# Row-wise dot products of two streamed arrays: another split of the last step between VectorE and ScalarE, other transfer sizes at its end, and all sums of six steps on VectorE

## The chip, the cores and the metric

The kernel runs on one core of one Trainium2 chip. The metric is the device time of one execution in microseconds, the median of several runs. The core's engines named here are VectorE (DVE in the profile), ScalarE (ACT) and SyncE (SP, which issues most of the transfers). TensorE (PE) and GpSimd (POOL) do no work of the kernel's own. Sixteen DMA engines move data between HBM and SBUF.

## What is computed

`x` and `y` are float32 of shape (8, 4096, 512). For each batch the reference forms the full product `x @ y^T`, takes its diagonal and a softmax over the 4096 diagonal values:

```
gram = np.matmul(x, y.transpose(0, 2, 1))
diag = np.diagonal(gram, axis1=1, axis2=2)
diag = diag - diag.max(axis=-1, keepdims=True)
exp = np.exp(diag)
return (exp / exp.sum(axis=-1, keepdims=True)).astype(np.float32)
```

Only the diagonal is needed, so the kernel computes 8 x 4096 dot products of 512 elements, row of `x` with the same row of `y`, and then the softmax of each batch. It reads 134 MB and writes 0.13 MB.

## The kernel before

The 128 partitions hold four batches of 32 partitions each; a partition has 128 consecutive rows of its batch. So the eight batches are two sets of four, and a set is 128 rows per partition. The rows are worked on in eight **steps** (0 to 7) of 32 rows per partition, four steps to a set. One step's `x` or `y` is 16384 elements, 64 KB, per partition. The results of a set are the 128 columns of `diag[0]` or `diag[1]`.

**Buffers.** `x` has two buffers, `xs0` and `xs1`, used in turn; `y` has one, `ys`. All input goes through SyncE's queue in the order of the program. An `x` transfer of step t+2 waits until the sums of step t have read their buffer, a `y` transfer of step t+1 until the products of step t have read `ys`.

**Steps 0 to 5** (L133 to L144). ScalarE copies the last K = 6 rows of `y` into `side` (L136). VectorE multiplies rows 0 to 25 of `x` by `ys` in place (`products`, L78), which frees `ys` for the next transfer, then rows 26 to 31 by `side`. VectorE then sums rows 0 to 29 in one reduction (`sums`, L81), and ScalarE the last W = 2 rows, one instruction with an accumulator for each (`sums_act`, L86). After step 3 the first set's maximum and exponentials follow (`exps`), and in step 4 its normalization (`normalize`).

**Step 6** (L146 to L156). The same with other sizes: three products of 8, 9 and 15 rows, the middle one from a copy of `y` in the free end of the other `x` buffer. VectorE sums the last two rows and ScalarE the first 30.

**Step 7** (L159 to L187). Its rows arrive in pieces, `x` and `y` in turn: x 15 rows, y 17, x 8, y 9, x 6, y 3, y 1, in the loop that begins at L164. Behind each piece VectorE takes the rows of which both sides are then asked for, one fused product and sum for each (`dots` and `dot`, L89). After row 16 it takes the maximum over the 48 values that set 1's steps 6 and 7 have so far (`largest`, L106). Then come `x` from row 29 up to all but the last V = 320 elements of row 31 (L179), y row 30, y row 31, and the last V elements of `x` (L185). Row 31 is taken in two parts of 192 and 320 elements. The first part's sum is written into the element of `x`'s buffer behind the row; `ys` has a 1.0 there, so that the second dot product, over 321 elements, adds it.

**The end.** ScalarE copies the finished part of `diag[1]` to `met` (L189), a copy that nothing reads; it stands ahead of the exponential and takes ScalarE's waits for earlier results. SyncE writes the first set's results in six transfers (L192). Each waits until an earlier transfer of the same semaphore has landed; eight semaphores are used in turn, so which one a transfer waits for depends on its place in the order. Then come the maximum over the last values, over the 32 partitions of each batch (L100), exponential and sum (L113), sum over the 32 partitions, reciprocal and scaling (L119, L120), and the output of set 1 from ScalarE's queue (L194).

Of the kernel before, what the change touches and what calls it, by code (L numbers as in the profile page):

```python
# [11 lines left out]
def kernel(  # L12
# [6 lines left out]
    nc = tc.nc  # L19
    ctx.enter_context(tc.manual_schedule())  # L20
    f32 = mybir.dt.float32
    Alu = mybir.AluOpType
    Act = mybir.ActivationFunctionType
    X = mybir.AxisListType.X
    B, N, D = x.shape
    P = nc.NUM_PARTITIONS
    G = 32
    Q = P // G
    C = N // G
    R = 32  # L30
    H = R // 2
    K = 6
    W = 2
    F = H + 1
    L = 9
    E = 64
    V = 5 * D // 8
    U = D - V
    S = B // Q * (C // R)

# [6 lines left out]
    small = ctx.enter_context(tc.tile_pool(name="small", bufs=1))  # L47
# [6 lines left out]
    ys = yflat[:, : R * D].rearrange("p (r d) -> p r d", d=D)  # L54
    side = big.tile([P, K, D], f32, name="side")

    diag = [small.tile([P, C + 2 * i], f32, name=f"diag{i}") for i in range(B // Q)]
# [6 lines left out]
    def rows(t, r0, n):  # L64
        return xs[t % 2][:, r0 : r0 + n, :]

    def dots_of(t, r0, n):
        return diag[t * R // C][:, columns(t, r0, n)]

    def load_x(t, r0, n):  # L70
        nc.sync.dma_start(out=rows(t, r0, n), in_=xv[t * R // C, :, columns(t, r0, n), :])  # L71

    def load_y(t, r0, n):
        nc.sync.dma_start(out=ys[:, r0 : r0 + n, :], in_=yv[t * R // C, :, columns(t, r0, n), :])  # L74

    def products(t, r0, n, yt):
        xt = rows(t, r0, n)
        nc.vector.tensor_tensor(out=xt, in0=xt, in1=yt, op=Alu.mult)  # L78

    def sums(t, r0, n):  # L80
        nc.vector.tensor_reduce(out=dots_of(t, r0, n), in_=rows(t, r0, n), axis=X, op=Alu.add)  # L81

    def sums_act(t, r0, n):
        for r in range(r0, r0 + n):
            row = xs[t % 2][:, r, :]
            nc.scalar.activation(out=row, in_=row, func=Act.Copy, accum_out=dots_of(t, r, 1))  # L86

    def dot(xt, yt, out):
        nc.vector.scalar_tensor_tensor(  # L89
            out=xt, in0=xt, scalar=1.0, in1=yt, op0=Alu.mult, op1=Alu.mult, accum_out=out  # L90
        )

    def dots(t, r0, n):
        for r in range(r0, r0 + n):
            dot(xs[t % 2][:, r, :], ys[:, r, :], dots_of(t, r, 1))

    def over_quadrant(name, column, op, negate=False):

        got = small.tile([P, 1], f32, name=name)
        nc.vector.tensor_reduce(  # L100
            out=got, in_=column.to_broadcast([P, G]), axis=X, op=op, negate=negate, apply_transpose=True
        )
        return got

    def largest(out, d):
        nc.vector.tensor_reduce(out=out, in_=d, axis=X, op=Alu.max)  # L106

    def exps(i, d):
        mxp = small.tile([P, 1], f32, name=f"mxp{i}")
        largest(mxp, d)  # L110
        nmx = over_quadrant(f"nmx{i}", mxp, Alu.max, negate=True)
        sump = small.tile([P, 1], f32, name=f"sump{i}")
        nc.scalar.activation(out=res[i], in_=diag[i][:, :C], func=Act.Exp, bias=nmx, scale=1.0, accum_out=sump)  # L113
        return sump

    def normalize(i, sump):
        total = over_quadrant(f"sum{i}", sump, Alu.add)
        rc = small.tile([P, 1], f32, name=f"rc{i}")
        nc.vector.reciprocal(out=rc, in_=total)  # L119
        nc.vector.tensor_single_scalar(out=res[i], in_=res[i], scalar=rc, op=Alu.mult)  # L120
# [12 lines left out]
    for t in range(S - 2):  # L133
        load_x(t, 0, R)
        load_y(t, 0, R)
        nc.scalar.activation(out=side, in_=ys[:, R - K :, :], func=Act.Copy)  # L136
        if t == C // R:
            normalize(0, sump)
        products(t, 0, R - K, ys[:, : R - K, :])
        products(t, R - K, K, side)  # L140
        sums(t, 0, R - W)
        sums_act(t, R - W, W)
        if t == C // R - 1:
            sump = exps(0, diag[0])  # L144

    t = S - 2  # L146
# [13 lines left out]
    chained = xflat[t % 2][:, R * D : R * D + 1]  # L160
    late = R * D - V
    upto = {load_x: 0, load_y: 0}
    done = 0
    for load, n in (  # L164
        (load_x, H - 1), (load_y, F), (load_x, 8), (load_y, 9), (load_x, 6), (load_y, 3), (load_y, 1)
    ):
        load(t, upto[load], n)
        upto[load] += n
        both = min(upto.values())
        dots(t, done, both - done)  # L170
        done = both
        if done == F:
            largest(diag[1][:, C : C + 1], diag[1][:, C - 2 * R : C - R + H])

    first = (R - 3) * D
    xt = xflat[t % 2]
    xrow = xv[t * R // C].rearrange("p c d -> p (c d)")
    end = ((t % (C // R)) + 1) * R * D
    nc.sync.dma_start(out=xt[:, first : late], in_=xrow[:, end - R * D + first : end - V])  # L179
    dots(t, done, 1)  # L180
    load_y(t, R - 2, 1)
    dots(t, R - 2, 1)
    load_y(t, R - 1, 1)
    dot(xt[:, late - U : late], yflat[:, late - U : late], chained)
    nc.sync.dma_start(out=xt[:, late : R * D], in_=xrow[:, end - V : end])  # L185
    dot(xt[:, late : R * D + 1], yflat[:, late : R * D + 1], dots_of(t, R - 1, 1))

    met = small.tile([P, C - R], f32, name="met")
    nc.scalar.activation(out=met, in_=diag[1][:, : C - R], func=Act.Copy)  # L189

    for p, n in ((0, H), (H, H), (2 * H, H), (3 * H, H), (4 * H, 2 * H), (6 * H, 2 * H)):
        nc.sync.dma_start(out=ov[0, p : p + n, :], in_=res[0][p : p + n, :])  # L192
    normalize(1, exps(1, diag[1][:, C - R + H :]))
    nc.scalar.dma_start(out=ov[1], in_=res[1])  # L194


# [28 lines left out]
```

## Time and profile before

| | |
|---|---|
| median of 3 runs | 319.96 us (319.86 to 320.12) |
| span of the profiled execution | 318.4 us |
| VectorE busy | 241.7 us, 76% of the span |
| ScalarE busy | 49.8 us, 16% |
| HBM read, written | 134.22 MB, 0.13 MB; 422 GB/s over the span |

The profiled execution is one run more, and its span is from the first to the last instruction; a time of its own beside the span isn't given, so the median stands for it: 1.56 us lie around the span. In the rows of the profile, L78 is line 78 of the kernel before. A row of the order of time has the start in us, the duration in us, the engine (SPq is SyncE's queue), the line, the operation and "out<-in". In brackets stands how long the engine was idle before it and what ended that. A row of a group has the operation, its shapes, how often it ran, then busy us and mean ns of one, then the idle time before.

### The profile page before, as it was taken

The page shows a single profiled execution, that of the slowest core. Times are in us where ns is not written, and L with a number is a line of the kernel's source. Part 1 is how long each engine was busy: PE and PEld are TensorE (multiplying, and loading weights), DVE is VectorE, ACT ScalarE, POOL GpSimd, SP SyncE. Part 2 cuts the span into 40 slices and gives each one's busy share as a digit, 9 for nine tenths or more (in the row PEclk, how much of TensorE's full clock was granted, in tenths as well). Part 3 has the DMA queues.
Part 4 walks back from the last instruction along what each step waited for, and adds up shares of the span by engine and source line. Part 5 has one row for each costly group of instructions (what it writes and reads, how often), then busy time and mean ns, then how long its engine had stood idle before and what let it go on. Part 6 is the DMA issues. An engine that isn't in the chain of part 4 may idle for free.

```text
span 318.4 us, 320 instructions
## 1 busy us (share of the span) xinstructions
DVE 241.7 (76%) x101; ACT 49.8 (16%) x97; POOL 0.2 (0%) x4
## 2 busy tenths in 40 slices
DVE  0000079994899939999399994999939998499995
ACT  1000030100301003010020102101030100496700
POOL 0000000000000000000000000000000000000000
DMA  9999999999999999999999999999999999999993
GB/s 397 395 395 510 412 395 453 469 395 395 486 436 395 453 469 395 395 486 436 395 395 519 403 395 461 461 395 395 527 395 395 486 436 395 425 415 432 434 410 140
DMA packets 3970, 134.37 MB, mean 422 GB/s; under 512 B 512, under 2 KB 896, under 8 KB 1536
## 3 DMA queue, kind: packets, MB, share of 16 engines
q1 hardware_dynamic: 3824, 134.29, 97.9%
q10 hardware_dynamic: 144, 0.07, 0.1%
q14 instruction: 2, 0.02, 0.0%
HBM read 134.22 MB, written 0.13 MB: 422 GB/s over the span
## 4 chain that ended last, share of the span: by engine, by line
DMA 70%; DVE 28%; issue 0%; SPq 0%; ACT 0%; DVEq 0%
DMA ys<-in_y_dram 59%; DVE xs L78 28%; DMA xs<-in_x_dram 11%; DVE xs L89 0%; SPq L74 0%; SPq L71 0%; DVE res L120 0%; DVE nmx L100 0%; DVE sum L100 0%; ACT res L113 0%; DVE mxp L106 0%; DVE rc L119 0%; DVEq L78 0%; DVEq L89 0%; SPq L131 0%
## 5 line engine op out<-in xcount | busy, mean ns | idle before, releaser
L78 DVE TENSOR_TENSOR xs<-xs,ys 128x13312 f32<-128x13312 f32 (+2 forms) x8 | 96.7, 12091 | 70.3 <-DMA ys<-in_y_dram 70.3
L81 DVE TENSOR_REDUCE diag<-xs 128x30 f32<-128x15360 f32 (+1 forms) x7 | 98.1, 14020 | 0.2
L86 ACT ACTIVATE xs<-xs 128x512 f32<-128x512 f32 x42 | 25.9, 617 | 90.4 <-DVE xs L78 90.4
L136 ACT ACTIVATE side<-ys 128x3072 f32<-128x3072 f32 x6 | 16.6, 2763 | 124.5 <-DMA ys<-in_y_dram 124.5
L89 DVE SCALAR_TENSOR_TENSOR xs<-xs,ys 128x512 f32<-128x512 f32 (+2 forms) x33 | 20.0, 669 | 0.8 <-DMA ys<-in_y_dram 0.7
L78 DVE TENSOR_TENSOR xs<-xs,side 128x3072 f32<-128x3072 f32 x6 | 20.1, 3350 | 0.0
L86 ACT ACTIVATION_READ_ACCUMULATOR xs<-xs 128x1 f32 x42 | 7.8, 187 | 0.0
L150 ACT ACTIVATE xs<-ys 128x4608 f32<-128x4608 f32 x1 | 4.0, 4043 | 19.9 <-DMA ys<-in_y_dram 19.9
L113 ACT ACTIVATE res<-diag,nmx 128x128 f32<-128x128 f32 x2 | 0.8, 401 | 29.8 <-DVE nmx L100 29.8
L78 DVE TENSOR_TENSOR xs<-xs,xs 128x4608 f32<-128x4608 f32 x1 | 5.0, 4951 | 0.0
L89 DVE DVE_READ_ACCUMULATOR xs<-xs,ys 128x1 f32 x33 | 2.7, 81 | 0.0
L124 ACT ACT_TABLE_LOAD x1 | 1.3, 1283 | 0.7 <-PEq L209 0.7
L100 DVE TRANSPOSE_TENSOR_REDUCE sum<-sump 128x1 f32<-128x32 f32 x2 | 0.4, 212 | 1.2 <-ACT res L113 1.2
L128 DVE MEMSET ys<- 128x1 f32 x1 | 0.1, 59 | 1.4 <-PEq L209 1.4
L120 DVE TENSOR_SCALAR res<-res,rc 128x128 f32<-128x128 f32 x2 | 0.6, 286 | 0.1
L106 DVE TENSOR_REDUCE mxp<-diag 128x1 f32<-128x128 f32 (+1 forms) x2 | 0.5, 228 | 0.1
L100 DVE TRANSPOSE_TENSOR_REDUCE nmx<-mxp 128x1 f32<-128x32 f32 x2 | 0.4, 212 | 0.1
L106 DVE TENSOR_REDUCE diag<-diag 128x1 f32<-128x64 f32 (+1 forms) x2 | 0.4, 202 | 0.0
L119 DVE RECIPROCAL rc<-sum 128x1 f32<-128x1 f32 x2 | 0.3, 164 | 0.1
L113 ACT ACTIVATION_READ_ACCUMULATOR res<-diag,nmx 128x1 f32 x2 | 0.4, 186 | 0.0
L189 ACT ACTIVATE met<-diag 128x96 f32<-128x96 f32 x1 | 0.3, 282 | 0.0
L209 POOL MEMSET const-bfloat16-1.0<- 128x1 bf16 x1 | 0.1, 101 | 0.0
(3 smaller groups left out, 0.3 us busy)
## 6 DMA issues: line engine op xcount, KB each, us to landing
ys<-in_y_dram SPq DMA_DIRECT2D x1, 4352.0 KB, 14.8
xs<-in_x_dram SPq DMA_DIRECT2D x1, 3840.0 KB, 14.1
ys<-in_y_dram SPq DMA_DIRECT2D x1, 2304.0 KB, 12.2
xs<-in_x_dram SPq DMA_DIRECT2D x1, 2048.0 KB, 19.3
xs<-in_x_dram SPq DMA_DIRECT2D x1, 1536.0 KB, 15.5
ys<-in_y_dram SPq DMA_DIRECT2D x1, 768.0 KB, 16.9
ys<-in_y_dram SPq DMA_DIRECT2D x3, 256.0 KB, 18.2
xs<-in_x_dram SPq DMA_DIRECT2D x1, 608.0 KB, 18.0
```

Source lines behind the costliest of these rows:

```text
L78: nc.vector.tensor_tensor(out=xt, in0=xt, in1=yt, op=Alu.mult)
L81: nc.vector.tensor_reduce(out=dots_of(t, r0, n), in_=rows(t, r0, n), axis=X, op=Alu.add)
L86: nc.scalar.activation(out=row, in_=row, func=Act.Copy, accum_out=dots_of(t, r, 1))
L89: nc.vector.scalar_tensor_tensor(out=xt, in0=xt, scalar=1.0, in1=yt, op0=Alu.mult, op1=Alu.mult, accum_out=out)
L100: nc.vector.tensor_reduce(out=got, in_=column.to_broadcast([P, G]), axis=X, op=op, negate=negate, apply_transpose=True)
L106: nc.vector.tensor_reduce(out=out, in_=d, axis=X, op=Alu.max)
L113: nc.scalar.activation(out=res[i], in_=diag[i][:, :C], func=Act.Exp, bias=nmx, scale=1.0, accum_out=sump)
L119: nc.vector.reciprocal(out=rc, in_=total)
L120: nc.vector.tensor_single_scalar(out=res[i], in_=res[i], scalar=rc, op=Alu.mult)
L124: nc.scalar.preload_act_table(Act.Exp)
L136: nc.scalar.activation(out=side, in_=ys[:, R - K :, :], func=Act.Copy)
L150: nc.scalar.activation(out=spare, in_=ys[:, F - L : F, :], func=Act.Copy)
```

## The change

- In steps 0 to 5 VectorE sums all 32 rows; ScalarE's two row sums go.
- In step 7 rows 0 to 9 are no longer dot products: VectorE makes two products of five rows each (2560 elements), and ScalarE sums the ten rows.
- The y of rows 26 to 29 comes in one transfer of four rows instead of three and one.
- V, the part of row 31 that arrives last, is 256 elements instead of 320 (the first part 256 instead of 192).
- The maximum so far is taken after row 25 instead of row 16, so that the last one runs over 6 + 2 values instead of 16 + 2.
- `met` copies the ten columns of ScalarE's sums too.
- The first set's results go out in seven transfers instead of six.

```
-    V = 5 * D // 8
+    V = D // 2
+    A = 10
...
-        sums(t, 0, R - W)
-        sums_act(t, R - W, W)
+        sums(t, 0, R)
...
-    for load, n in (
-        (load_x, H - 1), (load_y, F), (load_x, 8), (load_y, 9), (load_x, 6), (load_y, 3), (load_y, 1)
-    ):
+    for load, n in ((load_x, H - 1), (load_y, F), (load_x, 8), (load_y, 9), (load_x, 6), (load_y, 4)):
         load(t, upto[load], n)
         upto[load] += n
         both = min(upto.values())
+        if done < A <= both:
+            for r in range(0, A, A // 2):
+                products(t, r, A // 2, ys[:, r : r + A // 2, :])
+            sums_act(t, 0, A)
+            done = A
         dots(t, done, both - done)
         done = both
-        if done == F:
-            largest(diag[1][:, C : C + 1], diag[1][:, C - 2 * R : C - R + H])
+        if load is load_x and done > F:
+            seen = done
+            largest(diag[1][:, C : C + 1], diag[1][:, C - 2 * R : C - R + seen])
...
-    dots(t, done, 1)
+    dots(t, R - 3, 1)
...
-    met = small.tile([P, C - R], f32, name="met")
-    nc.scalar.activation(out=met, in_=diag[1][:, : C - R], func=Act.Copy)
-
-    for p, n in ((0, H), (H, H), (2 * H, H), (3 * H, H), (4 * H, 2 * H), (6 * H, 2 * H)):
+    met = small.tile([P, C - R + A], f32, name="met")
+    nc.scalar.activation(out=met, in_=diag[1][:, : C - R + A], func=Act.Copy)
+
+    for p, n in ((0, H), (H, H), (2 * H, H), (3 * H, H), (4 * H, H), (5 * H, H), (6 * H, 2 * H)):
...
-    normalize(1, exps(1, diag[1][:, C - R + H :]))
+    normalize(1, exps(1, diag[1][:, C - R + seen :]))
```

## The prediction, made before the result was known

> **What bounds the kernel now.** I read the page's totals first, then the chain of waits, then the order of time in one step and at the end, then the landings of the last step's transfers.
>
> ```profile
> span 318.4 us, 320 instructions
> DVE 241.7 (76%) x101; ACT 49.8 (16%) x97; POOL 0.2 (0%) x4
> DMA  9999999999999999999999999999999999999993
> ```
>
> VectorE (DVE) is busy 76% of the span and ScalarE (ACT) 16%, but the 16 DMA engines stand at nine tenths or more in every slice but the last. The kernel is a stream of transfers with a short tail, so two questions decide: does the change open a gap in the stream, and what does it do to the tail?
>
> The profiled execution spans 318.4 us; the median of the runs is 319.96 us, 1.56 us more, which lies around the span. I leave that part as it is and add my sum to both.
>
> One step, in order of time (step 0's work, with the issues for steps 1 and 2):
>
> ```profile
> 56.17 0.33 SPq L74 DMA_DIRECT2D ys<-in_y_dram  x1
> 59.39 16.15 DVE L81 TENSOR_REDUCE diag<-xs 128x30 f32<-128x15360 f32 x1
> 75.61 0.33 SPq L71 DMA_DIRECT2D xs<-in_x_dram  x1
> 80.89 14.03 DVE L78 TENSOR_TENSOR xs<-xs,ys 128x13312 f32<-128x13312 f32 x1 [5.35 <-DMA ys<-in_y_dram]
> 269.53 0.33 SPq L71 DMA_DIRECT2D xs<-in_x_dram  x1
> ```
>
> SyncE issues the x of step 2 when the sums of step 0 are done, at 75.61. At that time the y of step 1 is still on its way: VectorE starts on it at 80.89, after 5.35 us of idling. So the queue has about 5 us of work when the next x is put behind it. The tightest place is the x for step 7, issued at 269.53, with the y of step 6 landing at 250.11 + 24.41 = 274.52 (next fence): a lead of 5.0 us.
>
> The end, from the chain of waits:
>
> ```profile
> 250.11 24.41 DMA ys<-in_y_dram
> ...
> 298.80 14.80 DMA xs<-in_x_dram
> ...
> 313.70 0.51 DVE xs L89 x2
> 314.23 0.18 DVE mxp L106
> ```
>
> The last transfer, x's last 320 elements, lands at 298.80 + 14.80 = 313.60; the last dot product starts at 313.70, and maximum, exponential, sum, scaling and the output follow it. All of that tail stays as it is in the change but for two sizes.
>
> Now the last step's transfers: SyncE's issues, then kilobytes and the time from issue to landing.
>
> ```profile
> 292.00 0.33 SPq L74 DMA_DIRECT2D ys<-in_y_dram  x1
> 292.38 0.43 SPq L71 DMA_DIRECT2D xs<-in_x_dram  x1
> 292.85 0.43 SPq L74 DMA_DIRECT2D ys<-in_y_dram  x1
> 293.33 0.43 SPq L74 DMA_DIRECT2D ys<-in_y_dram  x1
> 293.80 0.43 SPq L179 DMA_DIRECT2D xs<-in_x_dram  x1
> 294.75 0.43 SPq L74 DMA_DIRECT2D ys<-in_y_dram  x1
> ```
>
> ```profile
> ys<-in_y_dram SPq DMA_DIRECT2D x1, 2304.0 KB, 12.2
> xs<-in_x_dram SPq DMA_DIRECT2D x1, 1536.0 KB, 15.5
> ys<-in_y_dram SPq DMA_DIRECT2D x1, 768.0 KB, 16.9
> ys<-in_y_dram SPq DMA_DIRECT2D x1, 256.0 KB, 17.1
> xs<-in_x_dram SPq DMA_DIRECT2D x1, 608.0 KB, 18.0
> ys<-in_y_dram SPq DMA_DIRECT2D x1, 256.0 KB, 18.4
> ```
>
> Issue plus duration gives the landings: y 17-25 at 304.2, x 23-28 at 307.9, y 26-28 at 309.75, y 29 at 310.4, x 29 to 31 (part) at 311.8, y 31 at 313.15; x's last part at 313.6. Against them VectorE's dot products:
>
> ```profile
> 294.03 0.69 DVE L89 SCALAR_TENSOR_TENSOR xs<-xs,ys 128x512 f32<-128x512 f32 x1 [0.68 <-DMA ys<-in_y_dram]
> 308.24 0.68 DVE L89 SCALAR_TENSOR_TENSOR xs<-xs,ys 128x512 f32<-128x512 f32 x1
> 310.07 0.68 DVE L89 SCALAR_TENSOR_TENSOR xs<-xs,ys 128x512 f32<-128x512 f32 x1
> 313.20 0.36 DVE L89 SCALAR_TENSOR_TENSOR xs<-xs,ys 128x192 f32<-128x192 f32 x1
> ```
>
> Row 0 starts at 294.03, row 23 at 308.24, row 26 at 310.07: one row each (310.07 - 308.24) / 3 = 0.61 us. Row 23 starts 0.35 us after its x landed and row 26 0.3 us after its y: VectorE is a little behind the stream there. It has caught up at the end: row 31's first part starts at 313.20, right behind y 31 at 313.15.
>
> **The change part by part.** The durations:
>
> ```profile
> L78 DVE TENSOR_TENSOR xs<-xs,ys 128x13312 f32<-128x13312 f32 x6 | 84.2, 14025 | 65.2 <-DMA ys<-in_y_dram 65.2
> L78 DVE TENSOR_TENSOR xs<-xs,side 128x3072 f32<-128x3072 f32 x6 | 20.1, 3350 | 0.0
> L81 DVE TENSOR_REDUCE diag<-xs 128x30 f32<-128x15360 f32 x6 | 96.9, 16153 | 0.2
> L81 DVE TENSOR_REDUCE diag<-xs 128x2 f32<-128x1024 f32 x1 | 1.2, 1220 | 0.0
> L89 DVE SCALAR_TENSOR_TENSOR xs<-xs,ys 128x321 f32<-128x321 f32 x1 | 0.5, 496 | 0.1
> L106 DVE TENSOR_REDUCE diag<-diag 128x1 f32<-128x48 f32 x1 | 0.2, 196 | 0.0
> L86 ACT ACTIVATE xs<-xs 128x512 f32<-128x512 f32 x42 | 25.9, 617 | 90.4 <-DVE xs L78 90.4
> 300.12 0.28 ACT L189 ACTIVATE met<-diag 128x96 f32<-128x96 f32 x1
> ```
>
> *Steps 0 to 5, 32 rows summed by VectorE.* A reduction costs (16153 - 1220) / 14336 = 1.042 ns an element, so 1024 more cost 1.07 us, and each sum takes 17.22 us. SyncE issues the next x that much later. The queue still holds 5.2 - 1.07 = 4.1 us of work then, 3.9 us at step 7's x, and VectorE idles some 4.3 us instead of 5.35 before each y. I take nothing for it, since the stream covers it. If the queue needed more than 3.9 us of work ahead, the cover would be gone; that is the slow rival. ScalarE loses two sums a step that nobody waited for.
>
> *Ten rows as two products of 2560 elements.* A product costs (14025 - 3350) / 10240 = 1.0425 ns an element; from 3350, 512 elements fewer give 2.82 us: 5.64 for ten rows, against 6.1 as dot products. VectorE gains 0.46 us. The form of 2560 is not in the trace; its bounds are no gain (6.1) and ten rows at the bare rate, 5120 x 1.0425 ns = 5.34.
>
> *ScalarE's ten sums* come behind its 30 of step 6, which end at 300.1, where `met` starts now. At 0.617 us a row they end at 306.3. The maximum over the rows so far waits for them on VectorE, with rows 26 to 31 queued behind it; it is moved behind row 25, at 309.7 by the sum below, so ScalarE has 3.4 us to spare. I take nothing.
>
> *VectorE up to row 25.* 294.03 + 5.64 + 7 x 0.61 (rows 10 to 16) = 303.94; y 17-25 lands at 304.2, so rows 17 to 22 run from 304.24 to 307.90; x 23-28 has just landed; rows 23 to 25 end at 309.73, the maximum (0.196 for 48 values, 0.2 for its 58) at 309.93. Before, row 26 started at 310.07: 0.14 us gained of the 0.46, the rest lost in waiting for y 17-25.
>
> *y of rows 26-29 in one transfer.* Row 26 now waits for all four rows. Two transfers brought them from 307.9 to 310.4. At the pace of the 1536 KB ahead of them, 3.7 us, 1024 KB take 2.45, so 310.35; bounds 310.3 and 310.45. VectorE, ready at 309.93, waits until 310.37, 0.30 us later than row 26 starts now. Rows 26 to 30 need 5 x 0.61 = 3.05: 313.42. Each finds its data landed (x 29 at about 311.85, y 31 at 313.15).
>
> The landing of y 29 comes 0.65 us after y 26-28 and carries 256 KB; the 768 KB before it took 1.87, or 0.62 per 256 KB, so a transfer of its own cost at most 0.03 us here. [...]
>
> *Row 31 at 256.* The row of 192 elements took 0.36 and that of 321 0.496, 1.054 ns an element: the first half costs 0.43, from 313.42 to 313.85. The stream carries the same bytes: 32 KB more ahead of y 30 and as much less behind y 31, so the last landing stays at 313.5 to 313.6. The last dot product now waits not for that landing but for the half row: it starts 0.02 us behind it (as the maximum does behind the last dot product, 314.21 to 314.23) to 0.10 (as now behind the landing, 313.60 to 313.70). I take 0.06: 313.91 against 313.70, +0.21 us. It is 64 elements shorter, -0.067. The last maximum takes 8 values instead of 18, under -0.01 by 0.18 for 18 and 0.196 for 48.
>
> *Issue order and outputs.* One input transfer fewer and one output transfer more. The last x is issued in one go behind y 31, at about 295, instead of 298.80; it stands in the same place in a queue that is full, so it lands no earlier. The first output (8 KB) goes out at 298.8 behind it. The last three go out at landings up to 313.2, over 2 us before the final output. Nothing.
>
> Sum: +0.21 - 0.067 - 0.01 = +0.13 us: span 318.5, time 320.1 us.
>
> **The rivals.**
>
> *The queue runs dry (slower).* Each of the six x transfers issued behind a sum is 1.07 us later. It decides once the queue needs more than 3.9 us of work ahead. The least lead that the trace shows to be enough is 5.0 us; if that were needed, each issue would lose about 1.0 us of stream, six in all: 326 us. Partial cases lie between 320.7 and 326. Against it:
>
> ```profile
> out_dram<-res ACTq DMA_DIRECT2D x1, 64.0 KB, 1.6
> ```
>
> a transfer on idle DMA engines is issued, moved and landed in 1.6 us, so a lead of 3.9 should do.
>
> *A transfer of its own costs queue time (faster).* If all of the 0.65 us of y 29 came off, y 26-29 would land at 309.75, and the last x at 312.9. Then VectorE is the bound: row 26 at 309.93, row 31 at 312.98, its half to 313.41, the last dot product at 313.47: -0.23 - 0.08 = -0.31, 319.65 us. [...] Against this speak the 0.03 us worked out above.
>
> *The stream alone sets the end (a little faster).* If the chain of rows 26 to 30 is shorter than I think, the last dot product starts behind the landing at 313.55 as now: -0.05 - 0.08, 319.8 us.
>
> *The wide products are dearer.* They have 0.26 us until y 17-25 lands and 0.42 more until y 26-29; past 0.7 us in all each us counts in full, and an excess of 1.2 us gives 320.6. Against it: the rate above comes from six products of each size, some of them beside ScalarE's work.
>
> **How the numbers follow.** Forecast 0.75; stream alone 0.08; dearer transfers 0.06; queue dry 0.07; dearer products 0.04. A measurement of this kernel tells about 0.2%, 0.64 us, from no change: 319.32 to 320.6. Forecast, stream alone and dearer transfers lie inside it; I leave 0.03 of them for faster and 0.01 for slower. Faster 0.03, same 0.85, slower 0.12. Range: from 319.6 (VectorE as the bound) to 320.5 (the sum at its upper bounds, y 26-29 at 310.45 and 0.10 behind the half, is +0.27; the runs scatter by 0.26).
>
> **What would show it.** Right: the sums of 32 rows take 17.2 us with VectorE idle 4.3 us before each y; DMA at nine tenths in all slices; row 26 starting at a landing near 310.35 after about half a us of idling; the last dot product waiting for the half row before it, at 313.9. Wrong: a hole in the DMA row after each sum; products over 3 us; ScalarE's tenth sum after 309.8; the last landing away from 313.5.

## The result, and the profile after

The changed kernel takes 320.54 us (median of 13 runs, 320.17 to 320.75); the kernel before, beside it, 319.96 us (13 runs, 319.68 to 320.98). The ratio is 1.0017, 95% interval 1.0009 to 1.0025. So it is slower by some 0.54 us by the ratio, where +0.13 was forecast. That is inside the 0.2% that the forecast called no change, but clear of zero and 0.04 us above the range.

In the rows of the changed kernel the lines have moved: L72 and L75 load x and y, L79 is the wide product, L82 the reduction, L90 the dot product, L107 a maximum, L193 `met`. The page's totals:

```profile
span 318.8 us, 290 instructions
DVE 247.6 (78%) x83; ACT 47.9 (15%) x93; POOL 0.2 (0%) x4
DMA  9999999999999999999999999999999999999993
```

The span is 0.4 us longer, and the DMA row still shows nine tenths in every slice but the last: no hole is to be seen at that width of 8 us. The groups by form and the order of time around the first late x:

```profile
L82 DVE TENSOR_REDUCE diag<-xs 128x32 f32<-128x16384 f32 x6 | 103.3, 17220 | 0.2
L79 DVE TENSOR_TENSOR xs<-xs,ys 128x2560 f32<-128x2560 f32 x2 | 5.6, 2820 | 0.9 <-DMA ys<-in_y_dram 0.9
```

```profile
76.76 0.33 SPq L72 DMA_DIRECT2D xs<-in_x_dram  x1
80.90 14.03 DVE L79 TENSOR_TENSOR xs<-xs,ys 128x13312 f32<-128x13312 f32 x1 [4.17 <-DMA ys<-in_y_dram]
270.69 0.33 SPq L72 DMA_DIRECT2D xs<-in_x_dram  x1
```

Both durations are as worked out (17.22 and 2.82 us). The x of step 2 is issued at 76.76, 4.1 us ahead of VectorE's start on the y before it, where it was 5.3. Now the last step: SyncE's issues, kilobytes with the time to landing, and the end of the chain of waits.

```profile
292.93 0.43 SPq L75 DMA_DIRECT2D ys<-in_y_dram  x1
294.83 0.45 SPq L189 DMA_DIRECT2D xs<-in_x_dram  x1
```

```profile
xs<-in_x_dram SPq DMA_DIRECT2D x1, 3840.0 KB, 13.2
ys<-in_y_dram SPq DMA_DIRECT2D x1, 1024.0 KB, 17.7
xs<-in_x_dram SPq DMA_DIRECT2D x1, 128.0 KB, 19.0
```

```profile
292.93 17.73 DMA ys<-in_y_dram
310.65 0.02 issue
310.68 3.23 DVE xs L90 x11
313.90 0.19 issue
314.09 0.10 DVE xs L90
314.19 0.02 issue
314.21 0.45 DVE xs L90 x2
```

```profile
306.32 0.29 ACT L193 ACTIVATE met<-diag 128x106 f32<-128x106 f32 x1
310.25 0.21 DVE L107 TENSOR_REDUCE diag<-diag 128x1 f32<-128x58 f32 x1
```

The tail has the form that was forecast: ScalarE is through with the ten sums at 306.3, VectorE takes the maximum at 310.25 and then waits for y of rows 26 to 29; the last dot product, at 314.21, waits for the half row and not for its transfer, which lands at 294.83 + 19.0 = 313.8. But all of it is late: x of step 7 (3840 KB) lands at 270.69 + 13.2 = 283.9 instead of 269.53 + 14.1 = 283.6, y of rows 26 to 29 at 310.65 instead of 310.35, the last x at 313.8 instead of 313.5. So in this execution 0.3 us are lost before the last step's changed transfers begin, and this part isn't theirs.

### The profile page after: what moved, and what is told of

It is laid out like the page before. It is cut to its first block, busy times and chain, and to the rows that moved or that the text cites. A ratio compares the mean times of both kernels' runs of the same rounds, so it can differ in the third digit from the quotient of the medians.

```text
span 318.8 us, 290 instructions
## 1 busy us (share of the span) xinstructions
DVE 247.6 (78%) x83; ACT 47.9 (15%) x93; POOL 0.2 (0%) x4
## 4 chain that ended last, share of the span: by engine, by line
DMA 65%; DVE 33%; issue 1%; SPq 0%; ACT 0%; DVEq 0%
DMA ys<-in_y_dram 65%; DVE xs L79 32%; DVE xs L90 1%; SPq L72 0%; SPq L75 0%; DVE res L121 0%; DVE nmx L101 0%; DVE sum L101 0%; ACT res L114 0%; DVE mxp L107 0%; DVE rc L120 0%; DVEq L79 0%; SPq L132 0%; SPq L131 0%
## 5 line engine op out<-in xcount | busy, mean ns | idle before, releaser
L79 DVE TENSOR_TENSOR xs<-xs,ys 128x13312 f32<-128x13312 f32 (+3 forms) x10 | 102.3, 10237 | 65.0 <-DMA ys<-in_y_dram 65.0
L82 DVE TENSOR_REDUCE diag<-xs 128x32 f32<-128x16384 f32 (+1 forms) x7 | 104.5, 14934 | 0.2
L87 ACT ACTIVATE xs<-xs 128x512 f32<-128x512 f32 x40 | 24.5, 614 | 2.8 <-DVE xs L79 2.8
L79 DVE TENSOR_TENSOR xs<-xs,side 128x3072 f32<-128x3072 f32 x6 | 20.1, 3352 | 0.0
L90 DVE SCALAR_TENSOR_TENSOR xs<-xs,ys 128x512 f32<-128x512 f32 (+2 forms) x23 | 13.9, 663 | 0.7 <-DMA ys<-in_y_dram 0.6
L79 DVE TENSOR_TENSOR xs<-xs,xs 128x4608 f32<-128x4608 f32 x1 | 5.0, 4951 | 0.0
L90 DVE DVE_READ_ACCUMULATOR xs<-xs,ys 128x1 f32 x23 | 1.9, 81 | 0.0
L107 DVE TENSOR_REDUCE mxp<-diag 128x1 f32<-128x128 f32 (+1 forms) x2 | 0.5, 226 | 0.1
L107 DVE TENSOR_REDUCE diag<-diag 128x1 f32<-128x64 f32 (+1 forms) x2 | 0.4, 212 | 0.1
L193 ACT ACTIVATE met<-diag 128x106 f32<-128x106 f32 x1 | 0.3, 292 | 0.0
## 6 DMA issues: line engine op xcount, KB each, us to landing
xs<-in_x_dram SPq DMA_DIRECT2D x1, 3840.0 KB, 13.2
```

What stands on the lines that cost most here:

```text
L90: nc.vector.scalar_tensor_tensor(out=xt, in0=xt, scalar=1.0, in1=yt, op0=Alu.mult, op1=Alu.mult, accum_out=out)
```

## The experiments

**Theory Q** (queue): the x of step t+2 is put into the queue with too little work ahead of it, so some of the 16 DMA engines are held up at its start. **Theory T** (tail): all of the loss comes from the last step. All times below are medians with the kernel before run beside them; a ratio is that of all runs, not of the two medians, and has its 95% interval. A single profiled execution is a weaker witness: the end of y of step 6, up to which the last-step experiments are the kernel before, falls at 274.52 us in the profile of before and at 249.58 + 24.40 = 273.98 in the chain of waits of the last step alone:

```profile
249.58 24.40 DMA ys<-in_y_dram
```

So the times are taken from the medians, and the profiles say in which place something waits.

**The sums alone** (the kernel before, and in steps 0 to 5):

```
-        sums(t, 0, R - W)
-        sums_act(t, R - W, W)
+        sums(t, 0, R)
```

> The kernel before with one part of the change: VectorE sums all 32 rows in steps 0 to 5; the last step is as before. Theory Q (the x of step t+2 is put into the queue 1.07 us later, with some 4.1 us of work ahead of it instead of 5.2, and its first packets start late on some of the 16 DMA engines): x of step 7 (3840 KB) lands near 283.9 us instead of 283.6, the last transfer near 313.85 instead of 313.60, and the time is 0.25 to 0.3 us above before, 320.2. Theory T (all of the measured +0.5 us comes from the last step: row 26 waiting for y of rows 26 to 29, and what follows): landings as before, 319.96, ratio 1.000.

320.19 against 319.86 us, ratio 1.0012 (1.0004 to 1.0021): +0.33. In order of time, landing and chain:

```profile
76.72 0.33 SPq L71 DMA_DIRECT2D xs<-in_x_dram  x1
80.82 14.03 DVE L78 TENSOR_TENSOR xs<-xs,ys 128x13312 f32<-128x13312 f32 x1 [4.12 <-DMA ys<-in_y_dram]
```

```profile
299.07 14.80 DMA xs<-in_x_dram
313.87 0.03 issue
```

With the last step as it was, the last transfer lands at 313.87 us instead of 313.60. Theory T, which put this kernel at the level of before, falls as the whole cause.

**The last step alone** (the changed kernel with the lines above turned back).

> The changed kernel with ScalarE summing two rows again in steps 0 to 5, so only the last step is changed. Theory Q: landings as before (3840 KB at 283.6, last transfer near 313.55), row 26 starts near 310.37, the last dot product near 313.9, time +0.13 us on before as the prediction summed it, 320.1. Theory T: row 26 near 310.68 as in the changed kernel, time 320.5.

320.17 against 319.86, ratio 1.0012 (1.0003 to 1.0020): +0.31, so the last step costs something too. The forecast's +0.13 for it lies at the low end of the interval (0.04% against 0.03 to 0.20%).

**y in three and one** (the changed kernel, y 26 to 29 in two transfers):

```
-(load_x, 6), (load_y, 4)):
+(load_x, 6), (load_y, 3), (load_y, 1)):
```

> The changed kernel with y of rows 26 to 29 in two transfers again (three rows and one); one more input transfer, all else as changed. Theory Q: the stream is still late (last transfer near 313.85), but row 26 starts near 310.5 behind the maximum instead of 310.68 behind y of row 29, and the last dot product starts right behind its transfer, near 313.95 instead of 314.21: 320.3, 0.25 us under the changed kernel. Theory T: if row 26's wait is the whole loss, 319.9.

320.25 against 319.86, ratio 1.0012 (1.0004 to 1.0021): +0.39. Theory Q had 320.3; T's 319.9 lies just below the interval, whose low end is 319.99. The 0.25 us that Q expected to win back from the changed kernel are within the scatter and not shown by this run alone.

**Two rows twice** (the sums alone, and `sums(t, 0, W)` again behind them).

> The kernel before with VectorE summing all 32 rows in steps 0 to 5 and then the first two rows a second time (same result): the x of step t+2 is issued 2.3 us later than before, with some 2.9 us of work ahead of it. Theory Q: the loss grows steeply, more DMA engines start their first packets late; at least 0.5 us for each of six issues, 3 us in all, 323. Theory T: nothing, 319.96, since the queue is never empty by the issue times.

326.79 against 319.86, ratio 1.0207 (1.0180 to 1.0233): +6.9 us. The page's DMA and GB/s rows, and the order of time:

```profile
DMA  9899899999899999999999999999979999899992
GB/s 388 386 458 442 386 506 394 410 490 386 369 410 466 410 426 466 402 458 434 386 394 434 458 394 482 418 377 394 490 305 482 394 442 434 318 439 409 430 412 96
```

```profile
78.07 0.33 SPq L71 DMA_DIRECT2D xs<-in_x_dram  x1
81.02 14.03 DVE L78 TENSOR_TENSOR xs<-xs,ys 128x13312 f32<-128x13312 f32 x1 [2.98 <-DMA ys<-in_y_dram]
```

Now the holes show: eights and a seven in the DMA row, slices at 305 and 318 GB/s. x is issued 2.95 us ahead of the start on y, and the loss is 6.9 / 6 = 1.15 us for each of the six issues on average; in the sums alone, where x was issued 1.35 us earlier, it was 0.06. The loss isn't even. In this profile VectorE's starts on y of steps 1 to 6 are 41.4, 38.6, 41.6, 39.7 and 39.0 us apart, where a step without loss takes 38.6 to 38.7 (the profile of the merged y alone). A late y also puts off VectorE's start on it, so that the next x has 5.6 us of lead again; a lead given for a kernel is therefore that of the first of its six places.

**The last step with y in three and one** (the last step alone, with the edit of the three and one).

> The changed kernel with ScalarE summing two rows again in steps 0 to 5 and y of rows 26 to 29 in two transfers again; what is left of the change is the wide products, the split at 256, the later maximum and the outputs. Theory Q with the prediction's working of the last step: the stream is as before, row 26 starts near 310.0 behind the maximum, the last dot product right behind its transfer, 0.05 to 0.1 us earlier and 0.08 us shorter: 319.8, ratio 0.9996. A rival (the last step costs something in the stream by its own transfer sizes): 320.1 to 320.2 as in the last step alone.

319.95 against 319.86, ratio 1.0001 (0.9993 to 1.0010). Wide products, split at 256, later maximum and output order together neither cost nor gain anything that can be measured.

**The merged y alone** (the kernel before):

```
-(load_x, 6), (load_y, 3), (load_y, 1)
+(load_x, 6), (load_y, 4)
```

> The kernel before with one part of the change: y of rows 26 to 29 in one transfer (one input transfer fewer, all else as before). The prediction's working: row 26 starts near 310.37 instead of 310.07, the half of 192 elements near 313.42, the last dot product near 313.85 instead of 313.70: +0.15, 320.0 to 320.1, ratio 1.0005. If a transfer fewer frees the queue: 319.9 or less.

320.05 against 319.86, ratio 1.0007 (0.9999 to 1.0016): +0.19, an interval that just holds zero; +0.15 was expected. VectorE in order of time:

```profile
310.03 0.69 DVE L89 SCALAR_TENSOR_TENSOR xs<-xs,ys 128x512 f32<-128x512 f32 x1 [0.26 <-DMA ys<-in_y_dram]
313.10 0.35 DVE L89 SCALAR_TENSOR_TENSOR xs<-xs,ys 128x192 f32<-128x192 f32 x1
313.38 0.08 DVE L89 DVE_READ_ACCUMULATOR xs<-xs,ys 128x1 f32 x1
313.49 0.49 DVE L89 SCALAR_TENSOR_TENSOR xs<-xs,ys 128x321 f32<-128x321 f32 x1
```

Row 26 waits 0.26 us for the merged transfer, and from there to the half row nothing waits: 3.07 us for five rows, where 3.05 was reckoned. The stream gains next to nothing from one transfer fewer: from the landing of x 23 to 28 to the last landing it takes 5.70 us (307.50 to 313.20), in the kernel before 5.72 (307.88 to 313.60).

**ScalarE six rows** (the kernel before with 26 rows on VectorE and `sums_act(t, R - K, K)`).

> The kernel before with ScalarE summing six rows in steps 0 to 5 and VectorE 26, so that each x is issued 2.1 us earlier, with some 7.3 us of work ahead of it. Theory Q with a threshold between 4.1 and 5.2 us: no change, 319.9. If 5.2 us is still too little for some of the 16 DMA engines: the stream's end comes earlier, up to 0.3 us, 319.6.

320.03 against 319.86, ratio 1.0004 (0.9995 to 1.0012).

```profile
73.48 0.33 SPq L71 DMA_DIRECT2D xs<-in_x_dram  x1
81.55 14.03 DVE L78 TENSOR_TENSOR xs<-xs,ys 128x13312 f32<-128x13312 f32 x1 [8.15 <-DMA ys<-in_y_dram]
```

With 8 us of work ahead it is not measurably faster or slower: 5.3 us had been enough.

**Sums in halves** (the kernel before; the first run halves x of steps 0 to 6, the second of steps 2 to 6):

```
-        load_x(t, 0, R)
+        load_x(t, 0, H)
+        load_x(t, H, H)
...
-        sums(t, 0, R - W)
-        sums_act(t, R - W, W)
+        sums(t, 0, H)
+        sums(t, H, H)
```

> The kernel before with VectorE summing all 32 rows in steps 0 to 5, as in the change, but in two reductions of 16 rows, and x of steps 0 to 6 in two transfers of 16 rows, so that the first half is issued 8.6 us earlier than the whole would be. Theory Q: what costs is the lead, not that VectorE has more to sum; the first half has some 12.7 us of work ahead of it: landings as before, 319.9, ratio 1.000. Rival (the longer VectorE work itself slows the stream): 320.2 as with the sums alone.

320.34 against 319.86, ratio 1.0012 (1.0003 to 1.0020): +0.48.

> As the sums in halves on the kernel before, but x of steps 0 and 1 whole as before, so that the start of the stream is not touched; x of steps 2 to 6 in halves. VectorE sums all 32 rows in steps 0 to 5. Theory Q (the lead of the x transfers is what costs): as before, 319.9, ratio 1.000; no packet of a first x is late. Rival (VectorE's longer work, or ScalarE's missing sums, costs by itself): 320.2 as with the sums alone.

320.29 against 319.76, ratio 1.0017 (1.0008 to 1.0025): +0.53. Theory Q's number failed in both. The packet records of the trace give a cost that the expectation had left out: a packet of 64 KB takes 2.418 us of its DMA engine, two of 32 KB take 2 x 1.213 = 2.426, and with eight partitions to an engine that is 8 x 0.008 = 0.06 us for each x that is halved, 0.32 for five and 0.45 for seven, an estimate. So by it the edit pays most of its loss itself, and it can't tell lead from VectorE's work.

**The changed kernel again, and with halves and y in three and one.**

> The changed kernel unaltered, beside the others on one chip. Both theories: 320.5, ratio 1.0017; its parts, the sums alone (1.0012) and the last step alone (1.0012), add up to 1.002 at most if they are independent.

320.47 against 319.76, ratio 1.0018 (1.0009 to 1.0026): +0.71. The parts, +0.33 and +0.31, make up the whole.

> The changed kernel with the lead given back (sums in two reductions of 16 rows, x of steps 2 to 6 in halves) and y of rows 26 to 29 in two transfers: VectorE still sums all of steps 0 to 5, and the wide products, the split at 256 and the later maximum stay. Theory Q: 319.8 to 319.95, the level of the kernel before. Rival (the longer VectorE work costs by itself): 320.2.

319.96 against 319.76, ratio 1.0005 (0.9997 to 1.0014): +0.20, at the level of before within its interval and nearer to theory Q, with the halves' own cost in it. The rival's 320.2 is at the end of the interval, so it is the next experiments that decide.

**One row twice** (the sums alone, and `sums(t, 0, 1)` behind them).

> The kernel before with VectorE summing all 32 rows in steps 0 to 5 and then the first row a second time (same result): the x of step t+2 is issued 1.7 us later than before, with some 3.5 us of work ahead of it. Theory Q: between the sums alone (+0.33 at 4.1 us) and two rows twice (+6.9 at 2.9 us), nearer to the first: +1.5 us, 321.4.

322.84 against 319.76, ratio 1.0095 (1.0078 to 1.0112): +3.1 us, twice what was expected.

```profile
77.58 0.33 SPq L71 DMA_DIRECT2D xs<-in_x_dram  x1
81.14 14.03 DVE L78 TENSOR_TENSOR xs<-xs,ys 128x13312 f32<-128x13312 f32 x1 [3.59 <-DMA ys<-in_y_dram]
```

**ScalarE late**: up to here VectorE worked longer wherever the lead was shorter. These two kernels leave VectorE as before and hold the x buffer with ScalarE instead, by copies that nothing reads:

```
         sums(t, 0, R - W)
         sums_act(t, R - W, W)
+        for n in (K, K, K, K, K, 4):
+            nc.scalar.activation(out=side[:, :n, :], in_=rows(t, 0, n), func=Act.Copy)
```

> The kernel before (VectorE sums 30 rows, ScalarE two) with five copies of six rows of x and one of four rows on ScalarE behind its two sums in steps 0 to 5, into a buffer that is free; they only keep ScalarE reading the x buffer until some 1.0 us after VectorE's sum, so the x of step t+2 is issued as late as in the sums alone, with some 4.1 us of work ahead, while VectorE does what it did before. Theory Q: the same loss as the sums alone, +0.3 us, 320.15. Rival (VectorE's longer work costs by itself): 319.85, ratio 1.000.

320.18 against 319.84, ratio 1.0011 (1.0003 to 1.0020): +0.34.

```profile
60.67 15.87 ACT L144 ACTIVATE side<-xs 128x3072 f32<-128x3072 f32 x6
76.57 0.33 SPq L71 DMA_DIRECT2D xs<-in_x_dram  x1
80.81 14.03 DVE L78 TENSOR_TENSOR xs<-xs,ys 128x13312 f32<-128x13312 f32 x1 [5.22 <-DMA ys<-in_y_dram]
```

VectorE idles 5.22 us as before, and yet x goes out at 76.57, when ScalarE lets go. With six rows in the last copy too:

> The same with six copies of six rows on ScalarE, so that x is issued some 1.8 us later than before, with some 3.4 us of work ahead. Theory Q: the same loss as one row summed twice at about that lead, +3 us, 322.9. Rival: 319.85.

322.49 against 319.84, ratio 1.0094 (1.0065 to 1.0123): +2.65.

```profile
77.64 0.33 SPq L71 DMA_DIRECT2D xs<-in_x_dram  x1
80.93 14.03 DVE L78 TENSOR_TENSOR xs<-xs,ys 128x13312 f32<-128x13312 f32 x1 [5.12 <-DMA ys<-in_y_dram]
```

> The sums alone once more, beside ScalarE's late copies: 320.2, ratio 1.0012.

320.17 against 319.84, ratio 1.0010 (1.0001 to 1.0018): +0.33 again. The rival, VectorE's longer work, falls: the same lead gives the same loss whichever engine shortens it. That ScalarE's copies cost by themselves isn't excluded by a run of its own, but with six row sums a step instead of two ScalarE cost nothing measurable above. By lead (x issued to VectorE's start on the y ahead of it in the queue, at the first of the six places):

| lead, us | kernel | against before, us |
|---|---|---|
| 8.1 | ScalarE six rows | +0.17 (interval holds zero) |
| 5.3 | before | 0 |
| 4.2 | ScalarE late | +0.34 |
| 4.1 | the sums alone, twice measured | +0.33, +0.33 |
| 3.6 | one row twice | +3.1 |
| 3.3 | ScalarE later | +2.65 |
| 2.95 | two rows twice | +6.9 |

**Half the packets, same lead.** Why do 3 to 4 us of queued work not do? One thought, theory P: a packet of 64 KB occupies its DMA engine for 2.42 us, and an engine needs the descriptors (the orders for its next packets) while a whole packet is still to go. Theory L: the lead needed is a time, whatever the packets. So in one row twice and two rows twice y of steps 1 to 6 comes in halves of 32 KB per partition, issued one behind the other:

```
-        load_y(t, 0, R)
+        for r in range(0, R, H if t else R):
+            load_y(t, r, H if t else R)
```

> One row summed twice (x issued with some 3.6 us of work ahead, +3.1 us), with y of steps 1 to 6 in two transfers of 16 rows, issued one behind the other, so that the packets ahead of each x are of 32 KB (1.21 us) instead of 64 KB (2.42 us); the bytes ahead of x and the lead in us are as they were. The halves' own cost is 6 x 0.064 = 0.4 us. Theory P (a DMA engine must have its next descriptors while a whole packet is still to go, so the lead needed falls by some 1.2 us with the packet): the loss falls to the halves' own cost and little more, +0.4 to +0.8, 320.2 to 320.6. Theory L (the lead needed is a time, whatever the packets): +3.1 + 0.4, 323.3.

323.26 against 319.79, ratio 1.0109 (1.0092 to 1.0125): +3.5.

> Two rows summed twice (x issued with some 2.95 us of work ahead, +6.9 us), with y of steps 1 to 6 in two transfers of 16 rows as in the run beside it. Theory P: 2.95 us of lead over packets of 1.21 us is like some 4.15 us over packets of 2.42, where the loss was +0.33; with the halves' own 0.4, +0.7, 320.6. Theory L: +6.9 + 0.4, 327.

326.70 against 319.79, ratio 1.0219 (1.0201 to 1.0238): +6.9. The order of time of the second:

```profile
78.22 0.33 SPq L71 DMA_DIRECT2D xs<-in_x_dram  x1
81.05 14.03 DVE L78 TENSOR_TENSOR xs<-xs,ys 128x13312 f32<-128x13312 f32 x1 [2.86 <-DMA ys<-in_y_dram]
```

The lead, 2.83 us, is that of whole packets, and so are both losses; theory P, which wanted 320.6 at most, falls.

None of these kernels beats the kernel before. The nearest, the last step with y in three and one, is equal to it.

## Why the prediction was wrong

**The step that failed** is that of steps 0 to 5: "I take nothing for it, since the stream covers it." The duration was right (17.22 us, x issued 1.15 us later, lead 4.1), and the lead was read rightly. The price of nothing was wrong: at 4.1 us it is +0.33 us, shown by the sums alone twice and by ScalarE's late copies. The forecast's slow rival had this mechanism, with a point "once the queue needs more than 3.9 us of work ahead" and prices from 320.7; the cost begins earlier, between 5.3 and 4.1 us, and smaller.

**Why the evidence against the rival misled.** The forecast took the 1.6 us of a 64 KB output on idle DMA engines for the lead that is needed. It measures one transfer; the lead is needed on each of the sixteen engines. The landing records of the trace, one per DMA engine, show y of step 1 of the kernel before arriving over 0.59 us, so the first engines are out of work 0.6 us ahead of the last. The packet records of the changed kernel show who is held up: at 273.4 us, as the x of step 7 begins, three packets of 30 KB among the first six to begin take 0.70, 0.82 and 0.98 us more than the 1.14 of all others. At 234.8 four of 64 KB take 0.24 to 0.55 more than 2.42, also on engines that begin early; at 80.4 three take 0.25 to 0.40 more, and these are the last three to begin. In the kernel before no packet at these places takes 0.07 us more. An early engine's hold-up first uses up its own 0.6 us in hand, and only the rest can reach the last landing: after the hold-ups at 234.8 the next step takes 38.58 us, as one without loss. The last engines have nothing in hand: after the hold-ups at 80.4 the step takes 39.01 us. That this makes the loss small at first, 0.3 us in all, and steep as the lead shrinks, is argued from these few places.

How much lead would have done can be read from the same records. In the six profiles with about 4.1 us of lead (the changed kernel and the sums alone, twice each, y in three and one, ScalarE late) the first DMA engine comes to the x 2.6 to 3.3 us after its issue, and some of the x's first packets take over 0.2 us more than the others. The start of such a packet plus the time that it took too long is an estimate of when its engine was at full pace: 2.9 to 4.2 us after the issue. In the profiles of before, the last step alone, the last step with y in three and one, and the merged y alone, the first engine comes to it 3.8 to 4.4 us after the issue, and none of the first packets takes 0.2 us more. So an engine needs up to some 4 us from the issue, and the first engine is there about 1 us ahead of the last landing, to which the lead is counted. A lead of 5.3 us covers both, 4.1 does not.

**The last step** was forecast at +0.13 and measured at +0.31 (0.10 to 0.64), so its size is compatible and no more. Point by point: wide products 2.82 us each (2.82 forecast), ScalarE's sums done at 306.3 (306.3), maximum at 310.25 (309.73; 0.3 of the difference is the late stream, and 0.2 pass before the maximum begins behind row 25's sum, which the forecast had put at nothing), row 26 at 310.68 right behind its landing; five rows in 3.07 us (3.05); the last dot product right behind the half row, 314.21 (313.91, and 0.30 of that difference is the late stream). The merged y alone is +0.19 for 0.15 expected, its interval just holding zero, and without it the rest of the last step is +0.09 with an interval around zero. That the merge costs a wait and gains next to nothing in the stream was right: 0.03 us at most was allowed for a transfer of its own, and the stream gains 0.02.

**The other rivals.** "A transfer of its own costs queue time" falls with the merged y alone, whose stream is 0.02 us shorter and not 0.65. The wide products came at the price that was forecast. "The stream alone sets the end" did not happen either: the last dot product waits for the half row.

**What stays open** is why an engine needs up to some 4 us from the issue when the queue is full. At the start of the kernel, with idle DMA engines, about 1 us passes from an issue (0.83 us) to its first packet (1.85 us). Packets of half the size changed nothing, so one packet in hand isn't the rule. It is also open why the loss falls on some of the six places and not on others. No run settles either.

## What to carry to other kernels

In a kernel that is one long stream, idle time on the engine that releases a buffer isn't free slack: it is the queue's lead, and it has to be compared with the lead that the trace already shows to be enough, not with the time of one transfer. Here a cut from 5.3 to 4.1 us cost 0.33 us and the next half us cost 2.8 more, so a bound from the nearest shown row, 5.0 us, should have been kept in the range. And merging two transfers that different rows wait for moves the first rows' data to the end of the whole; if the engine behind has no time in hand, that wait (0.26 us here) is the price, to be set against what the merge saves in the stream (0.02 us here).

## What the runs showed of the hardware

- The onset is gradual and then steep: with x issued 5.3, 4.1, 3.6 and 2.95 us ahead of VectorE's start on what stands before it, the stream of 134 MB lost 0, 0.33, 3.1 and 6.9 us over six such places. With packets of half the size ahead of x, the last two were 3.5 and 6.9 us. At 4.1 us the DMA row of the page still showed nine tenths in every slice but the last.
- By estimate from the packet records, an engine was at full pace on a newly issued transfer up to 4.2 us after the issue when the queue was full, against about 1 us to the first packet with idle engines at the kernel's start.
- Single DMA engines are held up, and not the whole queue. In the profile of the changed kernel the landings of the x of step 7 are spread over 1.13 us on the sixteen engines, in that of before over 0.56, while the median engine landed at the same 283.2 us. A wide spread alone isn't the sign of it: the merged y alone has 0.83 us there and no packet held up.
- Packets of 64 KB and 32 KB differ by 0.008 us for the same bytes (2.418 against 2 x 1.213), by estimate 0.3 us in this stream when x of five steps is halved.
